# Mixer 1's decay-weighted products run once per pair of heads, their matrices in one ring of seven tiles

## The chip, the cores and the metric

The kernel runs on one core of a Trainium2 chip. The metric is the device time of one execution in microseconds (us); lower is better. Three timed executions of the kernel before gave 2629.65, 2632.46 and 2633.35 us, so the median is 2632.46 us.

## The reference, cut to what matters

The model has two layers. Layer 0 mixes 512 tokens (256 of context, 256 latent) with a bidirectional state-space scan, here called mixer 1, and then runs a dense SwiGLU; layer 1 has an RWKV mixer and a mixture of experts. Only the scan matters here. In chunks of 128 tokens, and for each of 32 heads of 64 columns and each direction, it computes

```python
lower = (pos[:, None] >= pos[None, :])[:, :, None, None]
seg = cum[:, :, :, None] - cum[:, :, None, :]
decay = jnp.exp(jnp.where(lower, seg, -jnp.inf))
cb = jnp.einsum('bcign,bcjgn->bcijg', cm, bm)
w = cb[..., None] * decay * dt[:, :, None]
y = jnp.einsum('bcijge,bcjgep->bcigep', w, x)
y = y + jnp.einsum('bcign,bcgepn->bcigep', cm, s_prev) * jnp.exp(cum)[..., None]
```

so that inside a chunk every head and direction has a 128x128 matrix of decays times `cb`, which is multiplied with the inputs scaled by dt; the state carried from other chunks adds the last line. Both directions are added up.

## The kernel before, in words

Activations lie transposed: channels on partitions, the 512 tokens on the free axis. Mixer 1 goes through 4 groups of 8 heads; `inputs(g)` projects B and C of a group and makes `cb` (128x512: four chunks side by side). Each group has two halves of 4 heads, and a half is `mix(g, s, ...)`: two tiles of 128 channels (m = 0, 1), each a pair of heads. So there are 16 pairs in all. Beside `mix` run the projections of x (`x_products`) and of the gate (`gate_z`), each 48 matrix multiplications of 128x512 on lines L217 to L219, with the cast of the weights into a high part (`whi`, L211, ScalarE) and a low part (`wlo`, L212, VectorE).

`mix` first convolves x, transposes it and scales it by dt into `xdt` (L516, one tile for each direction), then runs a chain over the chunks that builds the carried states `st` (POOL L527, TensorE L530, ScalarE L533, VectorE L535 and L538). Then for each pair of heads:

- For each direction d and each head e of the pair a decay matrix is made. TensorE writes exponents into a PSUM bank `pbc` (L549 and L550; two such banks), ScalarE takes four exponentials of 128x128 into a tile `E` (L555; two buffers), and VectorE multiplies `E` with `cb` into a tile `W` (L557; four buffers).
- After the two matrices of a direction, TensorE multiplies them with `xdt` into the PSUM bank `py` (L562): for each chunk c head 0 writes rows 0 to 63 and head 1 rows 64 to 127. Every such product of float32 operands is two instructions in the trace, so a direction has 4 x 2 x 2 = 16 instructions and a pair has 32.
- `py` is added to the output tile `yz` (L565).
- For each direction the part from the carried state is added: exponents again (L569), exponentials into another buffer of `E` (L572), products of the state with C (L577), `W` = E times that (L580), and an addition to `yz` (L581).

The tile framework orders the instructions of each engine when the kernel is built: a planner takes what is ready by its own modelled costs, with what stands earlier in the program ahead of what stands later. Each engine then runs its list in that order and waits at semaphores. A tile from a ring (`bufs=n`) can be written again only when every reader of its earlier use is done.

After mixer 1 its pools are closed. The output projection opens with casts of `yz` into `yhi` (L619) and `ylo` (L620), which TensorE's next products read.

Of the kernel before, what the change touches and what calls it, by code (L numbers as in the profile page):

```python
# [10 lines left out]
F32 = mybir.dt.float32  # L11
# [10 lines left out]
NT = 512  # L22
# [120 lines left out]
def tile_backbone(ctx: ExitStack, tc: tile.TileContext, T, out: bass.AP, dbg=None, stop=99):  # L143
    nc = tc.nc
    V, S, G, PE, SY = nc.vector, nc.scalar, nc.gpsimd, nc.tensor, nc.sync
# [18 lines left out]
    def bank(name, bufs):  # L164
        return ps.tile([128, 512], F32, name=name, bufs=bufs)
# [203 lines left out]
    yz = yzp.tile([128, 16, NT], F32, name="yz")  # L369
    ysq = Squares(rowp)  # L370
    with ExitStack() as es:
# [26 lines left out]
        mt = es.enter_context(tc.tile_pool(name="mt", bufs=2, reuse_waits="tile"))  # L398
# [7 lines left out]
        p = misc()  # L406
# [3 lines left out]
        v, e, q, q2, s, daTM = [part(i) for i in range(6)]  # L410
# [16 lines left out]
        for dst, ws in ((cum, ("tri_f", "tri_b")), (tail, ("tail_f", "tail_b")), (etot, ("ones", "ones"))):  # L427
            p = misc()
# [14 lines left out]
        for d in range(2):  # L443
            p = misc().bitcast(BF16)
# [28 lines left out]
        FIRST = (0, 1)  # L473
        LATE = ((0, 0), (0, 0), (0, 1), (2, 0))
        XE, ZE = (V,), (V,)
        ORDER = ((0, 1, 2, 3), (1, 0, 3, 2))
        def inputs(g):

            pbc = project(wsplit(T["w_mb"][5 * g]))
            bf = mt.tile([128, NT], F32, name="bf")  # L480
            cf = mt.tile([128, NT], F32, name="cf")
            conv(pbc[0], 16 + g, bf)
            conv(pbc[1], 20 + g, cf)
            pb = misc()
            for c in range(4):
                PE.transpose(pb[:, 128 * c:128 * c + 128], bf[:, 128 * c:128 * c + 128], ident)
            btm = mt.tile([128, 4, 128], F32, name="btm")
            S.copy(btm, pb.rearrange("p (c n) -> p c n", c=4))
            pc = misc()
            for c in range(4):  # L490
                sl = slice(128 * c, 128 * c + 128)
                PE.matmul(pc[:, sl], bf[:, sl], cf[:, sl], start=True, stop=True)
            cb = mt.tile([128, NT], F32, name="cb")
            S.copy(cb, pc)
            return bf, cf, btm, cb
# [5 lines left out]
        def mix(g, s, px, bf, cf, btm, cb):  # L501

            hf = 8 * g + 4 * s
            xdt = [mt.tile([128, 4, 256], F32, name=f"xdt{d}", bufs=1) for d in range(2)]
            xw = {}
            for m in range(2):
                mi = 4 * g + 2 * s + m
                xs = mt.tile([128, NT], F32, name="xs")
                conv(px[m], mi, xs)
                S.activation(yz[:, mi, :], xs, AF.Copy, scale=vc("mb_d", mi))  # L510
                p = misc()
                for c in range(4):
                    PE.transpose(p[:, 128 * c:128 * c + 128], xs[:, 128 * c:128 * c + 128], ident)
                for d in range(2):
                    sc_ = dtTM[:, :, 32 * d + hf + 2 * m:32 * d + hf + 2 * m + 2]
                    V.tensor_tensor(xdt[d][:, :, 128 * m:128 * m + 128].rearrange("p c (h q) -> p c h q", h=2),  # L516
                                    p.rearrange("p (c h q) -> p c h q", c=4, h=2),
                                    sc_.unsqueeze(3).to_broadcast([128, 4, 2, 64]), op=ALU.mult)

            st = [{}, {}]  # L520
            for d in range(2):
                prev = None
                hs = slice(32 * d + hf, 32 * d + hf + 4)
                for idx in range(3):
                    c = ORDER[d][idx]
                    xw = mt.tile([128, 4, 64], F32, name="xw")
                    G.tensor_mul(xw, xdt[d][:, c, :].rearrange("p (h q) -> p h q", h=4),  # L527
                                 etail[:, c, hs].unsqueeze(2).to_broadcast([128, 4, 64]))
                    p = misc()[:, :256]
                    PE.matmul(p, btm[:, c, :], xw, start=True, stop=True)  # L530
                    sn = mt.tile([128, 256], F32, name=f"st{d}{idx}", bufs=1)
                    if prev is None:
                        S.copy(sn, p)  # L533
                    else:
                        V.tensor_tensor(sn.rearrange("p (h q) -> p h q", h=4),  # L535
                                        prev.rearrange("p (h q) -> p h q", h=4),
                                        etot[:, c, hs].unsqueeze(2).to_broadcast([128, 4, 64]), op=ALU.mult)
                        V.tensor_add(sn, sn, p)  # L538
                    st[d][ORDER[d][idx + 1]] = prev = sn
            for m in range(2):  # L540
                mi = 4 * g + 2 * s + m
                py = bank("py", 1)
                for d in range(2):

                    Ws = []
                    for e in range(2):
                        h = hf + 2 * m + e
                        pbc = bank("pbc", 2)
                        PE.matmul(pbc, ehb[:, h:h + 1].to_broadcast([96, 128]), parts[d], start=True, stop=False)  # L549
                        PE.matmul(pbc, identb, maskb[:, d:d + 1, :].to_broadcast([128, 4, 128]),  # L550
                                  start=False, stop=True)
                        E = mt.tile([128, NT], F32, name="E")
                        for c in range(4):
                            sl = slice(128 * c, 128 * c + 128)
                            S.activation(E[:, sl], pbc[:, sl], AF.Exp, bias=ncum[:, c, 32 * d + h:32 * d + h + 1])  # L555
                        W = mt.tile([128, NT], F32, name="W", bufs=4)
                        V.tensor_mul(W, E, cb)  # L557
                        Ws.append(W)
                    for c in range(4):
                        sl = slice(128 * c, 128 * c + 128)  # L560
                        for e in range(2):
                            PE.matmul(py[64 * e:64 * e + 64, sl], xdt[d][:, c, 128 * m + 64 * e:128 * m + 64 * e + 64],  # L562
                                      Ws[e][:, sl], start=d == 0 and c == 0, stop=d == 1 and c == 3,
                                      skip_group_check=True)
                V.tensor_add(yz[:, mi, :], yz[:, mi, :], py)  # L565
                for d in range(2):
                    h = hf + 2 * m
                    pbc = bank("pbc", 2)
                    PE.matmul(pbc, ehw[:, h:h + 2, :].rearrange("p h q -> p (h q)"), parts[d],  # L569
                              start=True, stop=True)  # L570
                    E = mt.tile([128, NT], F32, name="E")
                    S.activation(E, pbc, AF.Exp)  # L572
                    p = misc()
                    cs = [c for c in range(4) if c != FIRST[d]]
                    for c in cs:
                        sl = slice(128 * c, 128 * c + 128)
                        PE.matmul(p[:, sl], st[d][c][:, 128 * m:128 * m + 128], cf[:, sl], start=True, stop=True)  # L577
                    W = mt.tile([128, NT], F32, name="W", bufs=4)
                    for sl in ((slice(128, 512),) if d == 0 else (slice(0, 128), slice(256, 512))):
                        V.tensor_mul(W[:, sl], E[:, sl], p[:, sl])  # L580
                        V.tensor_add(yz[:, mi, sl], yz[:, mi, sl], W[:, sl])  # L581

        def gate_z(g, s):
            mod_some(1 if g < 2 else 0)
# [13 lines left out]
        for g in range(4):  # L598
            bc = inputs(g)
            for s in range(2):  # L600
                mix(g, s, x_products(g, s), *bc)
                late.append((g, s))
                while len(late) > LATE[g][s]:
                    gate_z(*late.pop(0))
# [180 lines left out]

    def products(W, units, x_at, nk=8):

# [330 lines left out]
    def invert(tp, un, zbank, slots={}):  # L1118
# [5 lines left out]
        def tile_(name, n):  # L1124
            nm, shape = slots.get(name, (name, [128, n]))
            t = tp.tile(shape, F32, name=nm)
            if len(shape) > 2:
                t = t.rearrange("p a b -> p (a b)" if len(shape) == 3 else "p a b c -> p (a b c)")
            return t[:, :n]
# [9 lines left out]

        E = tile_("M0", 1024).rearrange("p (n t) -> p n t", t=32)  # L1140
        Cq = [C.rearrange("p c h t -> p (c h) t") for C in un.Call]
# [303 lines left out]
    cb = ol.tile([128, 8], F32, name="cb")  # L1445
    xsq = Squares(ol, 256)
    W, OX, OH = [], [], {}
# [157 lines left out]
    if True:  # L1605
# [3 lines left out]
        for k0 in (0, 4):  # L1609
            p = misc()  # L1610
# [46 lines left out]
        p = misc()  # L1657
# [5 lines left out]
        p = misc()  # L1663
# [21 lines left out]
    with ExitStack() as es:  # L1685
# [8 lines left out]
        mt = es.enter_context(tc.tile_pool(name="mt2", bufs=2, reuse_waits="tile"))  # L1694
# [175 lines left out]
```

## Time and profile before

| | us |
|---|---|
| median of three timed executions | 2632.46 |
| profiled execution, its own time | 2633.91 |
| its span, first to last instruction | 2632.1 |
| TensorE busy | 2440.6 (93%) |
| VectorE busy | 2018.5 (77%) |
| ScalarE busy | 1429.5 (54%) |
| GpSimd busy | 332.1 (13%) |

The profile is of one execution. Busy times are unions of instructions on an engine; TensorE's ends are modelled, and its matrix multiplications are pipelined, so that the distance from one start to the next says more than a duration. The pair loop of mixer 1 lies between 96 and 460 us of the span; the output projection, the SwiGLU, the RWKV mixer and the experts follow.

### The profile page before, as it was taken

To read this page: it belongs to the slowest core of one execution; us is meant where nothing else is said; L and a number is where in the kernel's file an instruction comes from. 1 tells how busy PE (TensorE), PEld (TensorE's weight loads), DVE (VectorE), ACT (ScalarE), POOL (GpSimd) and SP (SyncE) were. 2 spreads that over 40 slices of the span, in tenths; PEclk is the share of its full clock that TensorE was granted. 3 is DMA by queue.
4 is the path that set the end of the run, shared out by engine and by line. 5 is a ranking of instruction groups with operands and counts; after the bars stand their busy time and mean duration, and the time that the engine had idled before them with its cause. 6 is when DMAs were issued, how large, how long until landed. Compare 5 with 4: busy or idle time off the path is not lost. (4 is left out here: it accounts for less than half of the span.)

```text
span 2632.1 us, 44733 instructions
## 1 busy us (share of the span) xinstructions
PE 2440.6 (93%) x17802; PEld 1986.5 (75%) x17802; DVE 2018.5 (77%) x3037; ACT 1429.5 (54%) x2178; POOL 332.1 (13%) x416
## 2 busy tenths in 40 slices
PE   7999998999999979769879798999999999999997
PEld 4777775878888867658768587887888788878875
DVE  5787888667554276788675656999999899989997
ACT  4354445333222264436233235877787777878775
POOL 1011102010000145224432111000000000000001
PEclk9999999999999978678889698999999999999999
DMA  7323231435565222012020126899999899989993
GB/s 263 121 81 101 76 112 62 138 117 196 168 200 159 73 89 75 7 61 97 18 73 3 59 103 253 322 358 341 360 373 352 327 362 367 362 317 367 369 339 154
DMA packets 99266, 511.79 MB, mean 194 GB/s; under 512 B 11688, under 2 KB 19112, under 8 KB 55272
## 3 DMA queue, kind: packets, MB, share of 16 engines
q1 hardware_dynamic: 97576, 506.68, 53.9%
q8 instruction: 141, 2.31, 0.4%
q10 hardware_dynamic: 1472, 2.16, 0.3%
q14 instruction: 77, 0.63, 0.1%
HBM read 506.71 MB, written 2.10 MB: 193 GB/s over the span
## 5 line engine op out<-in xcount | busy, mean ns | idle before, releaser
L1727 DVE TENSOR_TENSOR wlo<-wraw,whi 128x1024 fp32r<-128x1024 f32 x662 | 798.1, 1223 | 71.8 <-ACT whi L1726 50.6
L1726 ACT CAST whi<-wraw 128x1024 fp32r<-128x1024 f32 x662 | 694.5, 1051 | 207.2 <-PE gu L219 112.6
L218 PE MATMUL gu<-wlo,xg 128*128 128x512 f32 x896 | 355.3, 397 | 1.9 <-DVE wlo L1727 1.2
L219 PE MATMUL gu<-whi,xg 128*128 128x512 f32 x896 | 349.8, 390 | 0.0
L217 PE MATMUL gu<-whi,xg 128*128 128x512 f32 x896 | 336.3, 391 | 0.0
L211 ACT CAST whi<-wraw 128x1024 fp32r<-128x1024 f32 (+2 forms) x126 | 129.7, 1030 | 218.4 <-PE acc L218 206.1
L212 DVE TENSOR_TENSOR wlo<-wraw,whi 128x1024 fp32r<-128x1024 f32 (+2 forms) x126 | 151.0, 1199 | 109.7 <-ACT whi L211 109.5
L218 PEld LDWEIGHTS gu<-wlo,xg 128*128 128x128 f32 x896 | 168.5, 188 | 42.4 <-DVE wlo L1727 6.0
L217 PEld LDWEIGHTS gu<-whi,xg 128*128 128x128 f32 x896 | 168.4, 188 | 36.5 <-ACT xg L1746 0.4
L219 PEld LDWEIGHTS gu<-whi,xg 128*128 128x128 f32 x896 | 168.7, 188 | 31.6
L218 PE MATMUL y<-wlo,HT 128*128 128x512 f32 x448 | 178.6, 399 | 2.3 <-DVE wlo L1727 2.1
L217 PE MATMUL y<-whi,HT 128*128 128x512 f32 x448 | 176.7, 396 | 3.0 <-DVE xg L1747 3.0
L219 PE MATMUL y<-whi,HT 128*128 128x512 f32 x448 | 176.1, 393 | 0.0
L217 PE MATMUL acc<-h2hi,whi 128*128 128x512 f32 x352 | 137.4, 393 | 3.4 <-ACT h2hi L348 3.4
L218 PE MATMUL acc<-h2lo,whi 128*128 128x512 f32 x352 | 137.2, 391 | 0.0
L217 PE MATMUL acc<-hhi,whi 128*128 128x512 f32 (+1 forms) x328 | 135.7, 414 | 0.8 <-ACT whi L211 0.8
L1801 POOL TENSOR_TENSOR wraw<-yx,SH 128x512 f32<-128x512 f32 x4 | 7.5, 1877 | 1021.9 <-DVE yx L1797 1021.9
L219 PE MATMUL acc<-h2hi,wlo 128*128 128x512 f32 x352 | 134.7, 391 | 0.2
L218 PE MATMUL acc<-hlo,whi 128*128 128x512 f32 (+1 forms) x328 | 134.1, 409 | 0.0
L219 PE MATMUL acc<-hhi,wlo 128*128 128x512 f32 (+1 forms) x328 | 133.5, 408 | 0.0
L310 POOL TENSOR_TENSOR sqa<-sqa,sq 128x512 f32<-128x512 f32 (+1 forms) x35 | 47.6, 1360 | 579.5 <-issue 310.9
L777 POOL TENSOR_TENSOR wlo<-wraw,whi 128x512 fp32r<-128x512 f32 (+1 forms) x69 | 86.9, 1268 | 151.9 <-ACT whi L776 140.5
(566 smaller groups left out, 5226.3 us busy)
## 6 DMA issues: line engine op xcount, KB each, us to landing
wraw<-in_w_mi_dram SPq DMA_DIRECT2D x219, 1024.0 KB, 5.2
wraw<-in_w_mo_dram SPq DMA_DIRECT2D x112, 1024.0 KB, 5.5
wraw<-in_w_modT_dram SPq DMA_DIRECT2D x56, 512.0 KB, 3.7
wraw<-in_w_ffi_dram SPq DMA_DIRECT2D x44, 512.0 KB, 3.6
wraw<-in_w_mod_dram SPq DMA_DIRECT2D x40, 512.0 KB, 4.9
wraw<-in_w_mb_dram SPq DMA_DIRECT2D x40, 512.0 KB, 4.8
wraw<-in_w_mbo_dram SPq DMA_DIRECT2D x16, 512.0 KB, 4.1
wraw<-in_w_ffo_dram SPq DMA_DIRECT2D x16, 512.0 KB, 3.6
```

What stands on the lines that cost most here:

```text
L211: S.copy(hi, raw)
L212: eng[q % len(eng)].tensor_sub(lo, raw, hi.bitcast(F32))
L217: PE.matmul(o, whi, xhi, start=start, stop=False)
L218: PE.matmul(o, whi, xlo, start=False, stop=False)
L219: PE.matmul(o, wlo, xhi, start=False, stop=stop)
L310: G.tensor_add(self.acc, self.acc, sq)
L777: self.eng[self.n % len(self.eng)].tensor_sub(lo, raw, hi.bitcast(F32))
L1726: S.copy(hi, raw[:, k:k + 2, :])
L1727: V.tensor_sub(lo, raw[:, k:k + 2, :], hi.bitcast(F32))
L1801: G.tensor_mul(xf[:, tt, 512 * n:512 * n + 512], fs, fg[:, 512 * n:512 * n + 512])
```

## The change

The products of a pair (L562) no longer run once after each direction. All four matrices of the pair are made first, direction 0 then direction 1, and then one loop of 32 instructions runs over both directions, with direction 1 ahead of 0 and head 1 ahead of head 0, so that the first one reads the matrix that is made last. The multiplication with `cb` writes into the tile of the exponentials, and the part from the carried states does the same; the rings `E` (two buffers) and `W` (four) become one ring of seven. No instruction is added or taken out.

```diff
--- before.py
+++ after.py
@@ -473,6 +473,7 @@
         FIRST = (0, 1)
         LATE = ((0, 0), (0, 0), (0, 1), (2, 0))
         XE, ZE = (V,), (V,)
+        EB = 7
         ORDER = ((0, 1, 2, 3), (1, 0, 3, 2))
         def inputs(g):

@@ -540,27 +541,28 @@
             for m in range(2):
                 mi = 4 * g + 2 * s + m
                 py = bank("py", 1)
+                Ws = {}
                 for d in range(2):
-
-                    Ws = []
                     for e in range(2):
                         h = hf + 2 * m + e
                         pbc = bank("pbc", 2)
                         PE.matmul(pbc, ehb[:, h:h + 1].to_broadcast([96, 128]), parts[d], start=True, stop=False)
                         PE.matmul(pbc, identb, maskb[:, d:d + 1, :].to_broadcast([128, 4, 128]),
                                   start=False, stop=True)
-                        E = mt.tile([128, NT], F32, name="E")
+                        E = mt.tile([128, NT], F32, name="E", bufs=EB)
                         for c in range(4):
                             sl = slice(128 * c, 128 * c + 128)
                             S.activation(E[:, sl], pbc[:, sl], AF.Exp, bias=ncum[:, c, 32 * d + h:32 * d + h + 1])
-                        W = mt.tile([128, NT], F32, name="W", bufs=4)
-                        V.tensor_mul(W, E, cb)
-                        Ws.append(W)
+                        V.tensor_mul(E, E, cb)
+                        Ws[d, e] = E
+
+
+                for d in (1, 0):
                     for c in range(4):
                         sl = slice(128 * c, 128 * c + 128)
-                        for e in range(2):
+                        for e in (1, 0):
                             PE.matmul(py[64 * e:64 * e + 64, sl], xdt[d][:, c, 128 * m + 64 * e:128 * m + 64 * e + 64],
-                                      Ws[e][:, sl], start=d == 0 and c == 0, stop=d == 1 and c == 3,
+                                      Ws[d, e][:, sl], start=d == 1 and c == 0, stop=d == 0 and c == 3,
                                       skip_group_check=True)
                 V.tensor_add(yz[:, mi, :], yz[:, mi, :], py)
                 for d in range(2):
@@ -568,17 +570,16 @@
                     pbc = bank("pbc", 2)
                     PE.matmul(pbc, ehw[:, h:h + 2, :].rearrange("p h q -> p (h q)"), parts[d],
                               start=True, stop=True)
-                    E = mt.tile([128, NT], F32, name="E")
+                    E = mt.tile([128, NT], F32, name="E", bufs=EB)
                     S.activation(E, pbc, AF.Exp)
                     p = misc()
                     cs = [c for c in range(4) if c != FIRST[d]]
                     for c in cs:
                         sl = slice(128 * c, 128 * c + 128)
                         PE.matmul(p[:, sl], st[d][c][:, 128 * m:128 * m + 128], cf[:, sl], start=True, stop=True)
-                    W = mt.tile([128, NT], F32, name="W", bufs=4)
                     for sl in ((slice(128, 512),) if d == 0 else (slice(0, 128), slice(256, 512))):
-                        V.tensor_mul(W[:, sl], E[:, sl], p[:, sl])
-                        V.tensor_add(yz[:, mi, sl], yz[:, mi, sl], W[:, sl])
+                        V.tensor_mul(E[:, sl], E[:, sl], p[:, sl])
+                        V.tensor_add(yz[:, mi, sl], yz[:, mi, sl], E[:, sl])

         def gate_z(g, s):
             mod_some(1 if g < 2 else 0)
```

## Rows read from the trace of the kernel before

**Rows 1.** The page's head: the span, and each engine's busy time

```profile
span 2632.1 us, 44733 instructions
PE 2440.6 (93%) x17802; PEld 1986.5 (75%) x17802; DVE 2018.5 (77%) x3037; ACT 1429.5 (54%) x2178; POOL 332.1 (13%) x416
```

**Rows 2.** Windows: length, then busy by engine, granted clock, DMA share, GB/s

```profile
96.00:440.00 344.00, 339.16 (x2003) 249.41 (x2002) 277.50 (x503) 174.28 (x419) 55.92 (x60) 0.99 0.24 80
440.00:460.00 20.00, 12.39 (x81) 8.83 (x80) 17.42 (x29) 11.24 (x28) 4.16 (x3) 0.96 0.40 136
...
459.00:465.00 6.00, 6.00 (x18) 4.99 (x19) 6.00 (x9) 6.00 (x11) 0.68 (x1) 0.50 0.74 313
```

**Rows 3.** Timeline of TensorE, first pair: start, duration, line, tiles, count

```profile
106.35 0.39 PE L218 MATMUL acc<-hlo,whi 128*128 128x512 f32 x1
106.57 0.39 PE L219 MATMUL acc<-hhi,wlo 128*128 128x512 f32 x1
106.89 0.87 PE L562 MATMUL py<-W,xdt 128*64 128x128 f32 x10
107.69 0.70 PE L530 MATMUL misc<-xw,btm 128*128 128x256 f32 x2
108.32 0.43 PE L562 MATMUL py<-W,xdt 128*64 128x128 f32 x2
108.68 0.70 PE L530 MATMUL misc<-xw,btm 128*128 128x256 f32 x2
109.31 1.31 PE L562 MATMUL py<-W,xdt 128*64 128x128 f32 x20
110.56 0.60 PE L569 MATMUL pbc<-parts,ehw 96*128 96x512 bf16 x2
```

**Rows 4.** The same view, runs of 14 and 16, the last run and what follows

```profile
133.55 1.09 PE L562 MATMUL py<-W,xdt 128*64 128x128 f32 x14
134.57 0.39 PE L569 MATMUL pbc<-parts,ehw 96*128 96x512 bf16 x1
...
149.31 1.09 PE L562 MATMUL py<-W,xdt 128*64 128x128 f32 x16
150.34 0.50 PE L217 MATMUL acc<-hhi,whi 128*128 128x512 f32 x1
...
453.81 1.09 PE L562 MATMUL py<-W,xdt 128*64 128x128 f32 x14 [0.89 <-DVE W L557]
458.93 1.22 PE L217 MATMUL acc<-yhi,whi 128*128 128x512 f32 x2 [4.04 <-ACT yhi L619]
```

**Rows 5.** Line L562, 96 to 460 us: TensorE's idle time before it (us, times)

```profile
  issue: 10.4, 31
  DVE W L557: 6.4, 9
```

**Rows 6.** Waits of ScalarE, 96 to 460 us: total, times, longest

```profile
ACT E L555 <- DVE W L580: 33.0, 9, 8.5
ACT whi L211 <- PE acc L218: 24.1, 14, 3.3
```

**Rows 7.** Groups by line, 96 to 460 us: busy us, mean ns, idle before

```profile
L555 ACT ACTIVATE E<-pbc,ncum 128x128 f32<-128x128 f32 x256 | 72.3, 381 | 51.7 <-DVE W L580 33.0 <-PE pbc L550 14.5 <-DVE cv L460 2.4
L557 DVE TENSOR_TENSOR W<-E,cb 128x512 f32<-128x512 f32 x64 | 44.9, 709 | 8.3 <-ACT E L555 5.0 <-ACT cb L494 3.0
```

**Rows 8.** Timeline of ScalarE at the end of the stage

```profile
446.31 1.14 ACT L555 ACTIVATE E<-pbc,ncum 128x128 f32<-128x128 f32 x4 [4.64 <-DVE W L580]
```

**Rows 9.** Timeline of VectorE at the end of the stage

```profile
447.85 0.68 DVE L557 TENSOR_TENSOR W<-E,cb 128x512 f32<-128x512 f32 x1
...
452.52 1.23 DVE L557 TENSOR_TENSOR W<-E,cb 128x512 f32<-128x512 f32 x1 [0.45 <-ACT E L555]
...
455.01 0.68 DVE L565 TENSOR_TENSOR yz<-yz,py 128x512 f32<-128x512 f32 x1
```

## The prediction

> **What bounds the kernel now.** I read the page's head first, then the table of windows around the pair loop, then TensorE's own timeline, and last who waits for whom. The head says that TensorE is busy for 93% of the span and VectorE for 77% [rows 1]; that is a mean over stages, so I look at the stage that is changed. Between 96 and 440 us TensorE shows 339.16 us of 344, VectorE 277.50 (81%), ScalarE 174.28 (51%), at a granted clock of 0.99; in the last 20 us of mixer 1 the picture turns, with TensorE at 12.39 of 20 and VectorE at 17.42 [rows 2]. The reader is to see two stretches: a long one in which TensorE's list is the limit, and a short end in which it waits for VectorE.
>
> Busy time on TensorE may hide gaps, because its matrix multiplications overlap. The starts tell more: the products of 512 columns start 0.22 us apart (106.35 and 106.57 us) [rows 3], with a busy list on either side, so the engine is fed. What is not work in that list is switching. From the last projection to the first L562 it takes 0.32 us in place of 0.22 [rows 3], and before 31 runs of L562 TensorE stood idle for 10.4 us in all without waiting for anyone, against 6.4 us at nine places where it waited for a `W` [rows 5].
>
> **What a run of L562 costs.** A run is a row of L562 instructions with nothing else between; its cost is the start of the next instruction less its own start. 20 instructions take 110.56 - 109.31 = 1.25 us, 16 take 150.34 - 149.31 = 1.03, 14 take 134.57 - 133.55 = 1.02, 10 take 107.69 - 106.89 = 0.80, and 2 take 108.68 - 108.32 = 0.36 [rows 3, 4]. So four instructions (both heads of a chunk, side by side in the array) cost (1.25 - 1.03) = 0.22 us, a broken group costs as much as a whole one, and each run has a fixed 1.03 - 4 x 0.217 = 0.16 us on top. On TensorE's timeline the 512 instructions of the 16 pairs stand in 54 runs, the first at 106.89 and the last at 453.81 us [rows 3, 4]: 20 runs of 2, 2 of 6, 5 of 10 or 12, 19 of 14, 5 of 16, 3 of 18 or 20. Without waits that is 20 x 0.36 + 2 x 0.59 + 5 x 0.80 + 19 x 1.02 + 5 x 1.03 + 3 x 1.25 = 40.7 us. The runs of 2 followed by 14 come from the first loop's order: head 0's product of the first chunk is ready when one matrix is, and the rest waits for the second. Others are cut by the state chain (L530), as at 107.69 and 108.68 us.
>
> **The change, part by part.** The profiled execution took 2633.9 us, 1.4 above the median of the runs shown; the sum is made against 2633.9.
>
> *One loop of 32.* A whole pair costs 0.16 + 8 x 0.217 = 1.90 us, so 16 of them cost 30.4, which is 10.3 less. The first instruction now reads the matrix made last; when it may go, all 32 may, so the planner has no reason to start with two. Entering a run costs 0.32 - 0.22 = 0.10 us of its own, and 54 - 16 = 38 entries fewer give 3.8. Against this stands the state chain: it has the earlier place in the program, and for the first pair of each of the 8 halves it is still running. I keep one cut in each, at 0.16 + 0.10 and a broken group's part, some 0.3: 8 x 0.3 = 2.4 back. Together 10.3 + 3.8 - 2.4 = 11.7 us, on the engine that sets the end of this stretch. The nothing-gained end is 0 (54 runs again), the other end 14.1 (no cut).
>
> *Waits for the matrices.* Today 6.4 us at nine places [rows 5]. Tomorrow there are 16 places, and each waits for the last of four. The lower end is a gain of 6.4 (all ready in time). The upper one is that each block waits for a whole last matrix: four exponentials, 1.14 us [rows 8], and one multiplication, 0.71 [rows 7], 16 x 1.85 = 29.6, so 23.2 more than now. I take no difference, which is nearer to the row that exists: TensorE has projections to run while matrices are made, and the planner puts the block behind them as it does now. If it is behind this wait, what stands behind it on TensorE are the projections, and for those wait the convolutions.
>
> *One ring of seven.* ScalarE stood for 33.0 us at nine places because its next `E` was held until VectorE had done the carried-state product (L580), once for 8.5 us [rows 6]. With seven tiles, two for the carried state leave five for matrices, so this wait should go. I cost its going at nothing in the long stretch: ScalarE's casts wait 24.1 us for TensorE to give back their tiles [rows 6], so ScalarE is ahead there and the stall was covered. Its price if that cover is gone is the late tile: now a tile of the ring comes back only when TensorE has run the block, and behind a waiting exponential stand the weight casts. Bounds: 0 to the same 33 us of ScalarE time, which reach the end only beyond those 24.1 us, so 0 to 8.9 us; I take 0.
>
> *In place.* The multiplications keep their shapes: 64 x 0.71 us in L557 [rows 7]. The addition of `py` already writes the tile it reads and takes the same 0.68 us as an L557 beside it [rows 9]. I take no change. The bounds are those two rows: a few hundredths on 64 instructions on an engine with 19% free, under 2 us of its time either way and none of the end.
>
> *The end of the stage.* The last pair's first exponential waits 4.64 us for the tile, until 446.31 us [rows 8]. Its four multiplications (0.68, 0.68, 0.68 and 1.23 us) and the addition of `py` (0.68), 4.0 us in all, therefore fall after 447.85 us, when VectorE hardly stops and TensorE waits 4.04 us for the casts that follow [rows 4, 9]. With a free tile the matrices come before. They still cost VectorE their time, and it has little room there (17.42 of 20 us), so I take half, 2.0 us. The low end is 0. The high end is all 4.0, plus the clock: in 459 to 465 us TensorE ran 18 instructions at 0.50 granted, 1.2 GHz, having idled before it [rows 2, 4], and without that idle the same 18 products would take 18 x 0.22 = 4.0 of those 6 us, so 2.0 more.
>
> **Sum.** 2633.9 - 11.7 - 2.0 = 2620.2 us. Against the median it would be 1.4 less, which is inside the range; I say 2620. Later stages start earlier by what mixer 1 saves and their work is the same.
>
> **The rivals.**
>
> *TensorE is not the limit, and what it saves comes back as idle time.* VectorE at 81% is the next engine, and with two such engines under one order of work a shorter list on one may only wait for the other. For it: the last 20 us, where this is so. Against it: 339.16 of 344 us [rows 2]. It gives 2633.9, no change. The Trainium skill ("Trainium Kernel Development and Optimization", Performance Expectations) calls matmul busy time a bad measure, since matmuls are pipelined, and names the share of weight-load time as a good one. Weight loading is 249.41 of 344 us here, 73% [rows 2]; by that rule a quarter of TensorE would be free and this rival would be likelier than I make it. The distances of 0.22 us between starts [rows 3] speak for the busy list.
>
> *The planner cuts the block all the same.* If the state chain and the exponent products (L549, L569) go in between as often as to leave 40 runs, then 14 of 38 runs are saved, 14/38 x 14.1 = 5.2, and nothing at the end: 2628.7 us. For it: today's cuts by L530 within a block [rows 3]. Against it: most runs are short because of the order of the heads, which is removed.
>
> *Slower: the block stands in TensorE's list and waits.* A wait now serves 32 instructions and for the last of four matrices, and TensorE runs strictly behind it. At the full 1.85 us a block it costs 23.2 more, so 2633.9 - 11.7 - 2.0 + 23.2 = 2643.4 us. It decides from a mean wait of (6.4 + 13.7)/16 = 1.26 us a block. For it: VectorE's multiplications stand behind convolutions, and waits for `W` already exist. Against it: today's mean over nine is 0.7 us, and the ring lets the matrices be made well before.
>
> **How the numbers follow.** The measurement tells about 0.2%, 5.3 us, from no change: faster is below 2627.2 us, slower above 2637.7. The forecast, 2620 (its own range 2611 to 2627), gets 0.55; cut blocks, 2628.7, get 0.14; no gain, 2633.9, gets 0.18; slower, 2643.4, gets 0.13. Faster is the first and half of the second, 0.62. Slower is most of the last, 0.11. The rest, 0.27, is the same. The unknown costs together reach from 2633.9 - 14.1 - 6.4 - 6.0 = 2607.4 us to the slower rival; leaving out most of that rival and the last few us below, the range is 2609 to 2638.
>
> **What would show it.** Right: some 16 to 26 runs of L562, most of 32 at 1.9 us; ScalarE's wait for L580 gone or small; about the same 6 us of waits for the matrices; the output projection's first product about 12 to 14 us before 458.93. Wrong: waits of over 20 us for a matrix ahead of L562, TensorE well under 339/344 busy in the long stretch, or casts of weights that come late behind exponentials.

## The result, and the profile after

The changed kernel takes 2620.47 us (median of 7 runs, 2610.45 to 2622.45) beside 2632.46 (7 runs, 2628.49 to 2641.69): a ratio of 0.9947, 95% interval 0.9932 to 0.9961, 12.0 us less. The forecast was 2620. Its profiled execution took 2617.89 us.

The page's head after, for [rows 1], has the same work in a shorter span:

```profile
span 2616.0 us, 44690 instructions
PE 2433.9 (93%) x17802; PEld 1986.9 (76%) x17802; DVE 2019.2 (77%) x3037; ACT 1429.8 (55%) x2178; POOL 334.2 (13%) x416
```

The windows of mixer 1, for [rows 2], with the columns of that group; the stage now ends near 445 us, so its last 20 us are 426 to 446:

```profile
96.00:426.00 330.00, 327.75 (x2007) 244.22 (x2006) 275.41 (x500) 178.54 (x435) 57.67 (x60) 0.99 0.24 82
426.00:446.00 20.00, 13.36 (x80) 10.79 (x77) 17.85 (x33) 7.09 (x11) 5.37 (x4) 0.89 0.48 158
445.00:451.00 6.00, 5.87 (x18) 4.89 (x19) 5.81 (x9) 6.00 (x11) 0.88 (x1) 0.50 0.77 324
```

TensorE's timeline, for [rows 3, 4]: the first pair, a whole block, the last pair, and the first product of the output projection.

```profile
108.76 0.87 PE L564 MATMUL py<-E,xdt 128*64 128x128 f32 x10
109.56 0.70 PE L531 MATMUL misc<-xw,btm 128*128 128x256 f32 x2
110.19 1.52 PE L564 MATMUL py<-E,xdt 128*64 128x128 f32 x22
...
238.94 1.97 PE L564 MATMUL py<-E,xdt 128*64 128x128 f32 x32
240.83 0.39 PE L549 MATMUL pbc<-parts,ehb 96*128 96x512 bf16 x1
...
424.08 0.43 PE L564 MATMUL py<-E,xdt 128*64 128x128 f32 x2
424.44 0.70 PE L531 MATMUL misc<-xw,btm 128*128 128x256 f32 x2
425.07 1.53 PE L564 MATMUL py<-E,xdt 128*64 128x128 f32 x24
426.87 0.67 PE L531 MATMUL misc<-xw,btm 128*128 128x256 f32 x2 [0.27 <-DVE st L539]
427.47 0.65 PE L564 MATMUL py<-E,xdt 128*64 128x128 f32 x6
...
445.13 1.22 PE L217 MATMUL acc<-yhi,whi 128*128 128x512 f32 x2 [6.37 <-ACT yhi L620]
```

A block of 32 takes 240.83 - 238.94 = 1.89 us. There are 30 runs in place of 54, six of them whole; of the 14 cuts within a block the state chain (L531, which was L530) makes 10, products of the state with C (L579, which was L577) three and a transposition one. The last pair ran at 424 to 428 us; before, its last run began at 453.81 us [rows 4]. The output projection begins 458.93 - 445.13 = 13.80 us earlier. That is one pair of executions: two more with the same list of layer 0 as the kernel before (experiments below) begin it at 456.93 and 456.95 us, and one more with the list of the changed kernel at 444.64, so single pairs give 11.8 to 14.3.

Idle time ahead of the line, for [rows 5], its larger entries. No wait for a matrix is left:

```profile
  issue: 6.3, 19
  DVE wlo L212: 0.8, 2
```

This view adds up two rows of the trace, the multiplications (PE) and the loads of their weights (PEld), which overlap each other. In [rows 5] the 6.4 us are 5.5 of idle weight loading at eight places and 0.9 of the multiplications at one of the same eight, and the 10.4 us are weight loading alone. What TensorE lost by waiting stands in the waits of the multiplications. Before, 96 to 460 us, 8.0 us in all without the wait for `yhi`, and the weight loads' wait for `W`:

```profile
PE pbc L569 <- ACT E L555: 2.5, 4, 0.9
PE misc L577 <- DVE W L580: 1.7, 3, 1.2
PE misc L530 <- POOL xw L527: 1.5, 2, 0.8
PE py L562 <- DVE W L557: 0.9, 1, 0.9
...
PEld py L562 <- DVE W L557: 5.5, 8, 1.5
```

After, 96 to 450 us, 2.5 us in all, the two largest:

```profile
PE pbc L549 <- ACT E L555: 0.7, 1, 0.7
PE misc L531 <- POOL xw L528: 0.7, 1, 0.7
```

Waits of ScalarE, for [rows 6]. The 33.0 us for L580 are gone; in their place stand waits for the block (L564) and for the carried-state addition (L582), 20.8 us in the three rows shown. And ScalarE now waits 34.9 us for TensorE's exponents (L550), 14.5 before [rows 7]: it is ahead and TensorE is what it waits for.

```profile
ACT E L555 <- PE pbc L550: 34.9, 21, 3.7
ACT whi L211 <- PE acc L218: 27.2, 17, 3.6
...
ACT E L574 <- PE py L564: 11.3, 7, 3.0
...
ACT E L574 <- DVE yz L582: 4.8, 3, 2.8
ACT E L555 <- PE py L564: 4.7, 3, 2.5
```

The multiplication in place, for [rows 7]:

```profile
L556 DVE TENSOR_TENSOR E<-E,cb 128x512 f32<-128x512 f32 x64 | 44.6, 705 | 13.9 <-ACT E L555 13.6
```

VectorE's last product ahead of the output projection, before and after; the casts into `yhi` follow it:

```profile
456.85 0.69 DVE L594 SCALAR_TENSOR_TENSOR yz<-xs,yz 128x512 f32<-128x512 f32 x1
```

```profile
443.05 0.69 DVE L595 SCALAR_TENSOR_TENSOR yz<-xs,yz 128x512 f32<-128x512 f32 x1
```

### The profile page after: what moved, and what is told of

The parts are those of the page before. It is cut to its first block, busy times and chain, and to the rows that moved or that the text cites. A ratio compares the mean times of both kernels' runs of the same rounds, so it can differ in the third digit from the quotient of the medians.

```text
span 2616.0 us, 44690 instructions
## 1 busy us (share of the span) xinstructions
PE 2433.9 (93%) x17802; PEld 1986.9 (76%) x17802; DVE 2019.2 (77%) x3037; ACT 1429.8 (55%) x2178; POOL 334.2 (13%) x416
## 5 line engine op out<-in xcount | busy, mean ns | idle before, releaser
L265 DVE SCALAR_TENSOR_TENSOR wraw<-wraw,scb 128x1024 f32<-128x1024 f32 x56 | 68.7, 1226 | 49.6 <-DMA wraw<-in_w_modT_dram 48.9
```

Of the source, the lines that this page charges most:

```text
L265: V.scalar_tensor_tensor(t, w, 0.5, scb[:, j, :], op0=ALU.mult, op1=ALU.mult, accum_out=mods[l][:, n, j:j + 1])
```

## The experiments

**One part alone, whole kernels.** Theory A: the two parts, long blocks and long ring, each bring their share. Theory B: the ring alone brings the gain. Theory C: the loop alone. Four kernels, timed beside 2633.73 us of the kernel before.

The loop of 32 with the old rings:

```diff
-                        E = mt.tile([128, NT], F32, name="E", bufs=EB)
+                        E = mt.tile([128, NT], F32, name="E")
...
-                        V.tensor_mul(E, E, cb)
-                        Ws[d, e] = E
+                        W = mt.tile([128, NT], F32, name="W", bufs=4)
+                        V.tensor_mul(W, E, cb)
+                        Ws[d, e] = W
```

(against the changed kernel; the carried-state part gets its `W` back too)

> One loop of 32 over both directions, last-made matrix first, but with the two rings of the kernel before (E two buffers, W four). Planned list: 21 runs of L562 (54 before, 30 in the changed kernel). Theory A, two parts: run costs on TensorE and, apart from them, the ring (waits for W, the wait of the last pair's exponentials for L580). Then this kernel has the first part alone: runs 40.7 to 31.6 us, 33 entries fewer at 0.10, so about 12 less, with ScalarE's wait for L580 at 30 us or more and the end of the stage as before: 2620 to 2624 us, ratio 0.995 to 0.997. Theory B, the ring alone gives the gain: no change, 2632 us. Theory C, the loop alone gives it: 2618 to 2620, as the changed kernel or better.

Measured: 2641.41 us, ratio 1.0025 (1.0011 to 1.0040). A little slower; every theory missed. In its twelve executions the time goes with the granted clock of the whole execution: five at 0.935 to 0.937 took 2632.4 to 2635.2 us, seven at 0.925 to 0.933 took 2640.5 to 2650.0, all with one list.

The ring with the old loops:

```diff
-                        E = mt.tile([128, NT], F32, name="E")
+                        E = mt.tile([128, NT], F32, name="E", bufs=EB)
...
-                        W = mt.tile([128, NT], F32, name="W", bufs=4)
-                        V.tensor_mul(W, E, cb)
-                        Ws.append(W)
+                        V.tensor_mul(E, E, cb)
+                        Ws.append(E)
```

> The loop over each direction as before, but matrices in place in one ring of seven. Planned list: 55 runs of L562, so TensorE's run costs stay. Theory A: only the second part, the 6.4 us of waits for W and 4 us at the end of the stage: 2622 to 2628 us, ratio 0.996 to 0.998. Theory B, the ring alone: 2620 us, ratio 0.995. Theory C, the loop alone: 2632 us, ratio 1.000. A list built with the merged loop in the natural order (direction 0 first, head 0 first) is the same, instruction for instruction, on all five engines, so this run stands for that one too.

Measured: 2636.60 us, ratio 1.0016 (1.0005 to 1.0028). Theory B falls, and with it A as it stood.

The kernel before with the heads turned round:

```diff
-                        for e in range(2):
+                        for e in (1, 0):
                             PE.matmul(py[64 * e:64 * e + 64, sl], xdt[d][:, c, 128 * m + 64 * e:128 * m + 64 * e + 64],
```

> The kernel before with one edit: in each direction's loop head 1 goes ahead of head 0. Planned list: 34 runs of L562, 25 of them 16 long, own cost 33.4 us in place of 41. Theory A: the first part nearly whole, 7.5 us of run costs and 20 entries at 0.10, so 2622 to 2625 us, ratio 0.996 to 0.997, with the runs of 2 gone, and ScalarE's wait for L580 and the end of the stage as before. Theory B: 2632 us. Theory C (it needs one loop of 32): at most half, 2627 us or more.

Measured: 2632.15 us, ratio 0.9996 (0.9982 to 1.0010): no change, although in its profile the output projection began at 449.97 us, 9.0 earlier than before.

The changed kernel with a shorter ring:

```diff
-        EB = 7
+        EB = 6
```

> The changed kernel with a ring of six, the memory of the old rings. Planned list: 31 runs of L562. Theory A: two tiles for the carried state leave four for the next pair's matrices, enough to make all of them once the last pair's are given back, so within 2 us of the changed kernel, 2619 to 2623 us. Theory B, that the depth of the ring decides: ScalarE's waits for L564 or L582 rise well above 20 us and the time lies at 2626 us or more.

Measured: 2619.97 us, ratio 0.9944 (0.9928 to 0.9959), equal to the changed kernel. In its profile the output projection began at 444.82 us. The seventh tile does nothing that these runs can tell, and six tiles are as many as the old rings had together (two and four): what counts is not more tiles but one ring for both uses, with the product written in place. ScalarE waited 17.4 us for the block there, so that wait alone does not decide.

So the pieces did not add up, and the profiles showed a second place where time moved: from the first product of the RWKV mixer to the first expert product six kernels took 678.7 (changed kernel) to 692.0 us (loop with old rings), with the same work (the expectation below counts to a product some 5 us earlier). I therefore cut layer 1 off.

**The same kernels ended after layer 0.**

```diff
     mark("rwkv")
     mod_some(80)
+    SY.dma_start(out.rearrange("(p a) (k t) -> p (a k) t", p=128, t=256), X[:, :, 256:512])
+    return
```

> The kernel before, ended after layer 0 (layer 1 and the final norm are left out; the output is the stream after layer 0). Its lists of instructions up to there are those of the whole kernel. In the profiles the RWKV mixer took 673.7 to 687.0 us in six kernels in which it has the same work, so the whole times mix two effects. Theory D: the planner's list for layer 1 comes out a little different with every edit ahead of it, and that hides what mixer 1 does; then the four kernels of this kind differ as the starts of the output projection did. For this one about 940 us.

> The changed kernel ended after layer 0 (layer 1 and the final norm are left out). Theory D and the prediction's account: 12 to 15 us less than the kernel before that is ended at the same place. If the gain of the whole kernel came from layer 1's list: under 6 us less.

> One loop of 32, old rings, ended after layer 0 (layer 1 and the final norm are left out). Theory D: 1 to 4 us less than the kernel before ended at the same place, though its L562 stands in 21 runs and not 54: the run costs saved on TensorE (about 12 us) come back as waits, since with four W the next pair's matrices cannot be made before the block has run. If the whole kernel's 1.0025 is mixer 1's doing: 5 to 8 us more.

> Head 1 ahead of head 0 and nothing else, ended after layer 0 (layer 1 and the final norm are left out). Theory D: 7 to 10 us less than the kernel before ended at the same place: the runs of 2 are gone (own cost 41 to 33.4 us, 20 entries fewer at 0.10). If its 0.9996 in the whole kernel is mixer 1's doing: within 2 us.

> Ring of seven and in place, loops as before, ended after layer 0 (layer 1 and the final norm are left out). Beside 929.05 us of the kernel before and 915.26 of the changed one, ended there too. Theory E, the parts work only together: without the long ring a saved TensorE microsecond comes back as a wait for the next pair's matrices, without the long block the waits go but 55 runs of L562 remain. Then this one gives what the profile of the whole kernel showed at the output projection, 3 to 6 us less than 929.05, and loop (0) and ring (4) do not add up to 13.8. If the parts are independent it must give the rest, about 13 us less, since the loop alone gave none.

> The changed kernel with the matrices in a ring of six of their own and the carried-state part in a single tile of its own, ended after layer 0 (layer 1 and the final norm are left out). Planned list: 24 runs of L562 in place of 30, own cost 32.7 in place of 33.9 us. Theory E: the next pair's four matrices never stand behind L582, six are enough for them, so 912 to 916 us, equal to the changed kernel or up to 3 us better. If the depth kept for the carried state matters (one tile, so the second direction waits for the first direction's addition): 917 to 922 us.

The last one is, against the changed kernel:

```diff
-        EB = 7
+        EB = 6
...
-                    E = mt.tile([128, NT], F32, name="E", bufs=EB)
+                    E = mt.tile([128, NT], F32, name="Ec", bufs=1)
                     S.activation(E, pbc, AF.Exp)
```

Measured, medians of 5 runs, whose ranges lie apart, but for the loop with old rings, which meets its two neighbours. The last column is from the whole kernel beside its own runs of the kernel before. The last two rows were timed on another chip, where the kernel before took 0.1% longer; against that, the ratios give 2.9 and 10.0 us in place of the 2.5 and 10.0 of the medians.

| ended after layer 0 | us | range | less than before | whole kernel |
|---|---|---|---|---|
| before | 929.05 | 927.28 to 930.47 | | |
| changed kernel | 915.26 | 914.30 to 916.46 | 13.8 | 12.0 less |
| loop, old rings | 929.14 | 926.89 to 929.42 | -0.1 | 7.7 more |
| head order only | 923.32 | 922.74 to 923.98 | 5.7 | 1.6 less |
| ring only | 926.56 | 926.06 to 926.92 | 2.5 | 2.9 more |
| ring of six and one of its own | 919.01 | 918.87 to 919.93 | 10.0 | 15.4 less |

Two things follow. Layer 0 alone gains 13.8 us. In the two profiled executions of this pair it is 14.2, of which 12.3 lie ahead of the output projection (456.95 and 444.64 us) and 1.9 behind it, which no term explains. And loop alone (none) and ring alone (2.5) make 2.4 together, not 13.8: theory E holds for these two, which gain most of it only with each other. The head order alone, a piece of the loop's edit, gains 5.7 with the old rings, so it is joining the two directions that needs the one ring. Not tried: the loop with two rings that are each longer.

The expectations: the kernel before was 11 us under its 940; the loop (1 to 4 less) missed with none; head order (7 to 10 less) missed, 5.7; ring only (3 to 6) was close and a little high; that for the split ring (912 to 916) missed, and the other account, the depth kept for the carried state, gave the right size.

Why neither works alone can be read from the distances between TensorE's starts in mixer 1, from the first exponent product to the output projection, in the four kernels ended after layer 0. A distance counts for the instruction that starts it, so that a wait or a switch falls to the row of the instruction ahead of it (`py` is L562):

```
us                            before   loop,old rings   ring only   changed
py                             42.1         33.3           40.0       34.1
exponents (L549, L550, L569)   36.4         42.1           27.0       28.0
state times C (L577)           22.1         23.2           23.1       21.7
modulation (L248, L253)        16.4         19.5           18.6       17.2
projections (L217 to L219)    205.5        204.6          209.5      207.7
the rest                       33.7         33.5           32.9       33.2
idle before the first yhi       4.0          4.0            7.1        6.4
whole stage                   360.2        360.2          358.3      348.3
```

The changed kernel's stage is 11.9 us shorter here. The loop with old rings saves 8.8 us of `py`, and 5.7 of it come back at the exponent products, 3.1 at the modulation's products and 1.1 at L577. The waits of TensorE's multiplications, without the last for `yhi`, are 6.7 us before, 11.2 with the loop and old rings, 0.4 in ring only and 2.5 in the changed kernel. TensorE waits at the exponents for ScalarE to empty a bank, and ScalarE waits for a tile. The waits of ScalarE, loop with old rings, ended after layer 0:

```profile
ACT E L555 <- DVE W L583: 34.6, 14, 6.9
ACT E L575 <- PE pbc L572: 17.0, 8, 3.5
```

TensorE's waits in the same kernel:

```profile
PE pbc L572 <- ACT E L555: 5.6, 8, 1.2
```

L583 is the old L580. Its wait has not shrunk (31.2 us in the kernel before ended here), and the last pair of heads pays for it. ScalarE's timeline of this kernel at the last pair, and TensorE's:

```profile
441.18 1.14 ACT L555 ACTIVATE E<-pbc,ncum 128x128 f32<-128x128 f32 x4
443.38 3.48 ACT L555 ACTIVATE E<-pbc,ncum 128x128 f32<-128x128 f32 x12 [1.05 <-DVE W L583]
```

```profile
446.90 0.59 PE L572 MATMUL pbc<-parts,ehw 96*128 96x512 bf16 x1 [0.76 <-ACT E L555]
447.63 3.68 PE L565 MATMUL py<-W,xdt 128*64 128x128 f32 x32
455.29 1.22 PE L217 MATMUL acc<-yhi,whi 128*128 128x512 f32 x2 [3.98 <-ACT yhi L622]
```

```profile
440.00:450.00 10.00, 7.56 (x51) 5.31 (x52) 7.23 (x14) 7.23 (x21) 1.27 (x1) 0.82 0.28 100
450.00:460.00 10.00, 6.02 (x29) 4.93 (x26) 7.90 (x15) 6.00 (x10) 1.27 (x1) 0.50 0.56 209
```

The last pair's exponentials start at 441.18 us, and its block stands at 447.63 with no projection beside it. The block shows 3.68 us in place of 1.97: in its windows, shown last, TensorE had been idle for 2.44 of 10 us and the granted clock fell to 0.50, 1.2 GHz. In the changed kernel that block was done at 428. The same happens twice earlier, where the clock stood at 0.50 for 3.4 us after such pauses, from 391.83 and from 415.72 us. In the second, eight products of the projections start 0.43 us apart in place of 0.23, 1.6 us more, and the changed kernel has no such stretch between 100 and 440 us:

```profile
410.00:420.00 10.00, 7.87 (x32) 5.42 (x31) 9.53 (x19) 6.07 (x20) 1.63 (x2) 0.83 0.00 1
```

```profile
415.42 0.56 PE L217 MATMUL acc<-hhi,whi 128*128 128x512 f32 x1 [1.27 <-DVE xs L594]
415.77 0.63 PE L218 MATMUL acc<-hlo,whi 128*128 128x512 f32 x1
416.20 0.63 PE L219 MATMUL acc<-hhi,wlo 128*128 128x512 f32 x1
```

Ring only is the other half. Its windows: TensorE without a gap, at the old work.

```profile
96.00:445.00 349.00, 348.84 (x2064) 253.90 (x2065) 283.85 (x517) 180.21 (x438) 55.41 (x61) 0.99 0.25 81
```

```profile
  issue: 9.2, 29
```

The second fence is the largest entry of the idle time ahead of its L562: 29 entries that wait for nothing, and no wait for a matrix in the list. Of TensorE's 6.7 us of waits 0.4 are left, but 3.1 come back as a longer idle stretch at the end, and `py` gave only 2.1. Of the 9.4 us less at the exponents a good part is only a change of neighbours: a L562 stands right behind an exponent product 2 times and not 15, and a projection 56 times and not 36, 0.03 us behind it, with its own distance longer by about 0.2; so 4.0 us turn up at the projections. A TensorE without gaps and with 55 runs of L562 ends hardly sooner.

The split ring has fewer runs (24) than the changed kernel and is 3.8 us slower: with one tile for the carried state ScalarE waits 24.6 us for L582, and the last pair's block comes at 436.99 us. Its waits of ScalarE, and TensorE's timeline:

```profile
ACT Ec L574 <- DVE yz L582: 24.6, 13, 3.8
```

```profile
436.99 1.97 PE L564 MATMUL py<-E,xdt 128*64 128x128 f32 x32 [0.27 <-DVE E L556]
446.51 0.79 PE L217 MATMUL acc<-yhi,whi 128*128 128x512 f32 x1 [6.56 <-ACT yhi L620]
```

**Whole again, and the planner alone.**

> The same whole. Theory D: layer 1's list adds from -2 to +10 us to what layer 0 shows, so 2617 to 2630 us whatever layer 0 gives.

Measured: 2617.68 us, ratio 0.9945 (0.9930 to 0.9960), not to be told from the changed kernel, although layer 0 is 3.8 us slower. That is in the range for the whole, but theory D's step, -2 to +10 us, missed: behind layer 0 this kernel gained 5.4 us more. Neither this nor the ring of six beats the changed kernel by more than the measurement tells.

> The kernel before with one fence for the planner ahead of layer 1: nothing is reordered across it, and it issues no instruction and no wait. TensorE's and ScalarE's lists of layer 0 are those of the kernel before, so mixer 1 is the same; layer 1's list differs from TensorE's first product of the RWKV mixer on. Theory D: the time moves all the same, by 3 to 10 us, all of it between the first RWKV product and the first expert product. If lists in layer 1 do not matter: 2632 us, within 2.

```diff
     mod_some(80)
     ph.close()
+    tc.no_sync_barrier()
```

Measured: 2643.75 us, ratio 1.0038 (1.0024 to 1.0051), 10.7 us more, a little above the range expected. Two windows of the RWKV mixer, first of the kernel before, then of the fenced one, each from its own first RWKV product:

```profile
934.08:1191.78 257.70, 201.21 (x3001) 177.50 (x3001) 187.36 (x428) 119.45 (x273) 100.25 (x141) 0.78 0.16 52
1191.78:1615.16 423.38, 360.32 (x5788) 308.25 (x5787) 274.48 (x638) 161.59 (x375) 126.59 (x163) 0.83 0.23 82
```

```profile
931.98:1189.68 257.70, 202.60 (x2989) 179.14 (x2990) 187.39 (x427) 119.33 (x274) 101.43 (x141) 0.76 0.18 57
1189.68:1627.73 438.05, 368.42 (x5799) 315.13 (x5798) 272.37 (x638) 162.39 (x376) 129.15 (x163) 0.81 0.22 79
```

The first windows are of one length; by its end the fenced kernel is 1.4 us behind (the 3001st product starts at 257.7 us in the one and at 259.1 in the other), and the second window is 14.7 us longer, at a granted clock of 0.81 for 0.83. Of the 14.7 the profile of the whole keeps 9.8, since this execution reached the RWKV mixer 2.1 us earlier with the same list and was 2.8 us shorter behind it. So the loss does not sit at the fence but hundreds of microseconds behind it, where the instructions are the same and their order differs. Which swap costs it was not tried, nor how much of it the clock makes.

## Why the prediction was right, point by point

The time was right, and so was where it would show: 13.7 us were forecast, and the output projection began 13.80 us earlier in the profile, while layer 0 alone ended 13.8 us earlier. The terms of that sum were less good than the sum: they missed by -2.4 (loop), +5.5 (waits) and -4.3 us (end), with 1.3 not assigned, and that this cancels to 0.1 is luck. Of the signs that the prediction gave, the wait for L580 and the start of the output projection came true; 16 to 26 runs, most of them whole, did not (30, six whole).

*One loop of 32: forecast 11.7, found 9.3.* The price of a run was right (1.90 forecast for 32, 1.89 found). The number was not: 30 runs in place of 24, since a block is cut 14 times and not 8, 10 times by the state chain, and four times by products that the sum left out (L579, a transposition). `py` cost 40.7 us without waits and now 33.8 (34.1 with 0.3 of waiting at 425.07 us), so 6.9, and 24 entries fewer at 0.10 give 2.4.

*Waits for the matrices: forecast no change, found 0.9 gained here and 4.6 elsewhere.* All of [rows 5]'s waits are gone, but I had misread them: the 6.4 us are idle time of the weight loads for the most part, at eight places and not nine, while multiplications ran or waited for something else, and TensorE's multiplications waited 0.9 us for a `W`. Its other waits, which stood in no term, fell from 7.1 to 2.5 us: for a bank that ScalarE had not emptied (3.2 to 1.3), and for L580 itself (1.7 to none). The rival "slower" lived on this term and was not met.

*One ring of seven: forecast nothing.* This is the step that failed, though the sum did not show it. I said that ScalarE's 33 us for L580 were covered because its casts run ahead. In the kernel before most of them were, and ring only, without this wait, has 0.4 us of waits left on TensorE in place of 6.7. In the loop with old rings TensorE's list is shorter and they are not covered: ScalarE still waits 34.6 us for the product, TensorE 11.2, and these waits and the lower clock after them eat up what the loop saves. That the ring is the condition for the other term is shown: 0 without it, 13.8 with it, where the bounds of this term were 0 to 8.9 us. That it acts by this wait is read from the traces.

*In place: forecast nothing, found nothing.* 64 multiplications, 0.709 us each [rows 7] and 0.705 after.

*The end: forecast 2.0 gained, found 2.3 lost on TensorE.* TensorE's last work ahead of the output projection ended at 458.93 - 4.04 = 454.89 us, and now at 445.13 - 6.37 = 438.76, 16.1 earlier, which is 9.3 and 5.5 and 1.3 not assigned. But it then idles 6.37 us in place of 4.04, for the casts that wait for VectorE's last product, which ended at 457.54 and now at 443.74 us, 13.80 earlier; the granted clock after it is 0.50 as before. The matrices did leave the end, as I said. What I missed is that TensorE's end moved further than VectorE's, so the end of the stage is now VectorE's alone.

*The rivals.* "TensorE is not the limit" did not come true in the changed kernel, and the rule of the Trainium skill ("Trainium Kernel Development and Optimization", Performance Expectations) that would have made it likelier was a poor guide here: in ring only the weight-load share stays at 253.90 of 349, 73%, and yet TensorE's multiplications show no gap. But the rival's mechanism is what the loop with old rings shows: saved TensorE time back as idle time. "The planner cuts the block" came true in part.

*What stood in no term.* "Later stages start earlier and their work is the same" holds for the work, not for the time. Against 13.8 in layer 0, the whole kernel gained 12.0. The list of layer 1 is planned anew, and in five kernels the whole moved from 5.4 us less to 7.6 us more than layer 0 alone did (six and one: 15.4 for 10.0; loop with old rings: 7.7 more for 0.1 more), each with some 4 us of doubt by the intervals, and 10.7 with layer 0 unchanged. Part of it goes with the granted clock, with which one and the same list moves by as much (2632.4 to 2650.0 us above). That the changed kernel came out within 1.8 us is luck too, and a range that counted it would have been about 10 us wider on either side.

## What to carry to other kernels

A saving on the busiest engine is kept only if the next work is ready when that engine gets there: check which ring holds the work that should move up, and change both together. Read a saving from the waits of the multiplications and from the distances between starts, not from a view that adds the idle time of weight loads. In a kernel whose order a planner draws up, time an edit also with everything behind it cut off; the order that comes out behind an edit can be worth as much as the edit. To merge runs of instructions, turn the loop so that the first one needs the input that is made last: with the natural order the planner's list here was that of ring only, 55 runs of L562.

## What the runs showed of the hardware

- One head of a chunk alone costs TensorE as much as both heads side by side: a run of 2 takes 108.68 - 108.32 = 0.36 us [rows 3], and five runs of 4 in the changed kernel 0.37 each. In the loop with old rings, ended after layer 0, a block of 32 shows 1.97 us at a granted clock of 1.00, 2.4 GHz (from 407.91 us), and 3.68 at 0.50, 1.2 GHz (from 447.63).
- Each run of these half-width products costs a fixed 0.16 us, and 0.10 on entering, at a granted clock of 0.99 to 1.00: before, it starts 0.32 us after a projection's product in place of 0.23, 0.31 after an exponent product in place of 0.22, and 0.20 after a product of state with C in place of 0.11. The Trainium skill ("TensorEngine Tiling (Array Packing)", Key Properties) says that changing the tiling mode drains TensorE; the trace agrees as far as that there is a price, and no run here tells a drain from its other parts.
